# The two-input operations of GpSimd moved to VectorE, in a hybrid SSD and forgetting-attention block

## Chip, cores and metric

One core of a Trainium2 chip runs the whole layer in one launch. The metric is the device time of that launch in microseconds (us), the median of several runs. In the text PE is TensorE (matmuls), DVE is VectorE, ACT is ScalarE, POOL is GpSimd and SP is the SyncE queue that issues all DMAs.

## What is computed

Float32 throughout, one sequence of 1024 tokens, D = 1024. Cut to what matters:

```python
ada = silu(c) @ w_ada + b_ada;  shift, scale, gate = split(ada, 3)
h = rmsnorm(x, norm_w) * (1 + scale) + shift
z_ssm, xbc, dt_raw, q, k, v, z_att, f_logit, g_logit = split(h @ w_in)      # 8472 columns
# SSD branch: 16 heads of 64, 2 groups, state 64, chunks of 128 tokens
xs, bm, cm = split(silu(causal_conv(xbc)));  dt = softplus(dt_raw + dt_bias)
a_cs = cumsum(-exp(a_log) * dt) within a chunk
y = (cm bm^T * exp(a_cs[l] - a_cs[s])) (xs*dt)  +  cm state * exp(a_cs)  +  d_skip * xs
y_ssm = rmsnorm(y * silu(z_ssm), ssm_norm_w)
# attention branch: 8 heads of 128, causal, logits + f_cum[q] - f_cum[k]
y_att = softmax(q k^T * scale + forget) v * silu(z_att)
g_ssm, g_att = split(sigmoid(g_logit + b_gate))
merged = g_ssm * (y_ssm @ w_proj_ssm) + g_att * (y_att @ w_proj_att)
out = rmsnorm(x + gate * (merged @ w_out), final_norm_w)
```

## The kernel before

Every large product is made at nearly full float32 precision out of three matmuls. A tensor is *split* into a high part, which ScalarE casts (line 102), and a low part, raw minus high, a subtraction of two tensors in SBUF (line 103). Then high times high, high times low and low times high are summed in PSUM. `split(raw, hi, lo, n, eng)` takes the engine of the subtraction as an argument; in the kernel before its default is GpSimd. `unit` (line 87) loads a weight tile of 128 x 512 into one of four raw buffers (`wr`) and splits it into one of five `wh` and five `wl`.

The stages, in the order of time:

- **Start.** The tokens are normalised, the columns of w_ada are summed by VectorE (`ada_cols`, lines 287 and 289), and h is built, transposed and split into `hh` and `hl` (line 307). Three gate slabs fill TensorE meanwhile.
- **Half sums and pairs of slabs.** The columns of w_in come in slabs of 128. Two slabs at a time (`c_pair`, line 459) are multiplied with h in the manner of Strassen and Winograd: seven products instead of eight. `t_forms` (line 435) makes the sums and differences of h's halves once (`pe`, lines 440 to 444) and splits them (`tla`, `tlb`). For each pair VectorE forms four sums of weight tiles (lines 477 to 480), seven tiles are split (`wl`, and `sl` of three buffers), TensorE runs seven products of twelve matmuls, and VectorE adds the results up out of PSUM (lines 504 to 517). What follows depends on the slab: a tanh gate (`gt`, line 186), a silu (`zt`, line 525) or a causal convolution (`cv`, lines 538 to 544, four passes over 1024 columns on VectorE). Among the pairs a table, WPREP, places `w_sums` (line 575), which forms the weight sums of the later projections, and `out_gate` (lines 558 and 561), which forms the columns of the residual gate.
- **SSD.** Per quarter of the heads and chunk of 128 tokens (`ssd_half`, line 671): the decay matrix `ab` on ScalarE, its product with `cb` on VectorE (line 686), split into `m4`; xs transposed on TensorE, times dt (`xd`, line 700), times the decay (`xe`, line 703), both split into `xr`; the state `st32` updated (line 717) and split into `sn`; then the products. v and some q and k slabs run in between and fill TensorE.
- **Attention.** Per head and block of queries: logits on TensorE, the masked minimum on VectorE (line 1013), exp on ScalarE, normalisation on GpSimd (line 1021), transposes, split, product with v. GpSimd also selects the causal part (line 1004).
- **Projections.** `prod_c` runs three products (by w_proj_ssm, w_proj_att, w_out), again seven for eight, with `b_form` splitting the activations (`bl`), `w_in` (line 196) loading the weights, and `post` adding up. Sums of results (lines 1109 and 1126) and a product with the final norm's weight (line 1139) are GpSimd's. The end of each token block is a power on GpSimd (line 1144), two scalings and the store.

What sets the order: each engine runs its own queue in order, and a scheduler in the building layer puts the instructions of each queue into an order by its own estimate of when each can run, with a higher priority for the SSD and the attention. So an instruction that changes engine is put into the other queue where that estimate has it, and the order of the others can change with it. All DMAs are in SP's queue.

Which two-input operations were GpSimd's: every split whose call names no engine (the weights' `wl` and `sl`, `m4`, one half of `xr`, `sn`, v, spilled q and k), half of the sums and splits in `t_forms`, two sums and half of the gate products in `w_sums`, `xe`, the square sum `sacc` (line 778), and the sums and products named above. Two tables, WV and WVI (lines 54 and 55), gave some weight splits of the later projections to VectorE.

Of the kernel before, what the change touches and what calls it, by code (L numbers as in the profile page):

```python
# [27 lines left out]
ALU = mybir.AluOpType  # L28
# [25 lines left out]
WV = {'ps': (), 'pa': (1,), 'o': (1, 2, 3)}  # L54
WVI = (("o", 3),)
# [14 lines left out]
def build(ctx, tc, t):  # L70
# [16 lines left out]
    def unit(src, n, eng=G):  # L87
        raw = raw_tile()
        SP.dma_start(out=raw[:, :n], in_=src)
        return split(raw, hi_tile(), lo_tile(), n, eng)  # L90
# [10 lines left out]
    def split(raw, hi, lo, n, eng=G):  # L101
        A.copy(out=hi[:, :n], in_=raw[:, :n])  # L102
        eng.tensor_tensor(out=lo[:, :n], in0=raw[:, :n], in1=f32(hi[:, :n]), op=ALU.subtract)  # L103
        return hi, lo
# [91 lines left out]
    def w_in(n, i, p):  # L196
        if (n, i, p) in ws_scr:
            return unit(ws_scr[n, i, p], 512, V if p in WV[n] or (n, i) in WVI else G)
        return unit(t["w_" + n][p + 4 * (i == 4), i % 2 == 0 and 1 or 0], 512)
# [160 lines left out]
    with tc.tile_pool(name="pa", bufs=1, side="right") as pa, \  # L360
# [74 lines left out]
        def t_forms(k):  # L435
            th1, tl1, th2, tl2 = (pa.tile([P, S], F32R, name=f"t{n}{k}") for n in ("ha", "la", "hb", "lb"))
            b11, b12, b21, b22 = (pe_tile() for _ in range(4))
            lo, hi = slice(0, 512), slice(512, 1024)
            for b, kk, hs, eng in ((b11, k, lo, V), (b12, k, hi, G), (b22, k + 4, hi, G), (b21, k + 4, lo, V)):
                eng.tensor_tensor(out=b, in0=f32(hh[kk][:, hs]), in1=f32(hl[kk][:, hs]), op=ALU.add)  # L440
# [134 lines left out]
        def w_sums(n, p, gb=None):  # L575

            def raw_in(sl, u):
                x = raw_tile()[:, :512]
                SP.dma_start(out=x, in_=t["w_" + n][sl, u])
                if gb is not None:  # L580
                    (V if u else G).tensor_tensor(out=x, in0=x, in1=gb[:, 512 * (sl // 4):512 * (sl // 4) + 512],
                                                  op=ALU.mult)
                return x
# [4 lines left out]
            G.tensor_tensor(out=a21, in0=a11, in1=a21, op=ALU.subtract)  # L588
            G.tensor_tensor(out=s4, in0=a12, in1=s2, op=ALU.subtract)
# [40 lines left out]
    with tc.tile_pool(name="sd", bufs=1, side="right") as sd, \  # L630
# [40 lines left out]
        def ssd_half(qd, hf, xs, ys, st32, sn):  # L671
# [3 lines left out]
            for c in range(4 * hf, 4 * hf + 4):  # L675
# [25 lines left out]
                if c < NC - 1:  # L701
                    xe = sd.tile([P, 256], F32, tag="xe", bufs=2, name="xe")
                    G.tensor_tensor(out=h4(xe), in0=h4(xd), in1=hb4(dec), op=ALU.mult)
# [53 lines left out]
        for qd in range(4):  # L757
            st32, sn = sd.tile([P, 256], F32, tag="st32", bufs=1, name="st32"), None
            for hf in range(2):
# [7 lines left out]
                for i in range(2):  # L767
# [8 lines left out]
                    else:  # L776
                        A.activation(out=zt, in_=y, func=AF.Square)
                        G.tensor_tensor(out=sacc[:, hs], in0=sacc[:, hs], in1=zt, op=ALU.add)
# [75 lines left out]
    def b_t2(b11, b12, b22, b21=None):  # L854
# [5 lines left out]
        if b21 is not None:  # L860
            G.tensor_tensor(out=b21, in0=b21, in1=t2, op=ALU.subtract)
# [215 lines left out]
    with tc.tile_pool(name="finp", bufs=1, space=PSUM) as fpp_:  # L1077
# [9 lines left out]
        for i in OSSM:  # L1087
            if i in done_early:
                continue
            if i in (5, 4) and prep_u:  # L1090
                prep_u = False
                for p in range(4):
# [3 lines left out]
                    G.tensor_tensor(out=b[21][p], in0=b[21][p], in1=t2, op=ALU.subtract)  # L1096
# [8 lines left out]
        def att_done(ch, tk, p, ps):  # L1105
# [3 lines left out]
            G.tensor_tensor(out=m, in0=m, in1=gt, op=ALU.add)  # L1109
# [14 lines left out]
        def out_pre(hf, tk, p, st):  # L1124
            r = rt[4 * tk + p, hf]
            G.tensor_tensor(out=r, in0=r, in1=st, op=ALU.add)  # L1126

        def out_done(hf, tk, p, ps):
# [6 lines left out]
            if not last:  # L1135
# [3 lines left out]
                G.tensor_tensor(out=ra, in0=ra, in1=fw[:, hs], op=ALU.mult)  # L1139
# [101 lines left out]
```

## Time and profile before

| | |
|---|---|
| median of 3 runs | 1287.4 us (1284.27 to 1290.71) |
| profiled execution, its own time | 1286.09 us |
| its span | 1284.4 us |
| mean granted clock of TensorE | 0.974 |
| instructions of VectorE, GpSimd | 1618, 644 |

The span is that of one profiled execution; the rest of its time lies around it. A row of a group reads: line, engine, operation, what it writes and reads, shape, count, then busy time in all and the mean of one in ns, then the idle time of the engine just before these instructions and what ended it. Lines are those of the kernel before.

### The profile page before, as it was taken

Reading aid. Unit: us, or ns where it says so; the run is one execution under the profiler, and the core shown is the slowest. Engines: PE = TensorE matmul, PEld = TensorE weight load, DVE = VectorE, ACT = ScalarE, POOL = GpSimd, SP = SyncE. Lnnn points to the kernel's source line nnn. Section 1 sums busy time; section 2 is a strip of 40 time slices with the busy share of each in tenths; the row PEclk is TensorE's granted clock in tenths of the full one; section 3 lists DMA queues with packets and bytes.
Section 4 is the critical chain, followed back from the end, with each engine's and each line's share of the span. In section 5 each row is a group of like instructions: output and inputs, shape, how many; then the busy total and the mean of one; then the engine's idle time right before and its main releaser. Section 6 shows DMA issues by size and latency. Waiting matters only on the chain. (4 is left out here: it accounts for less than half of the span.)

```text
span 1284.4 us, 18783 instructions
## 1 busy us (share of the span) xinstructions
PE 1183.9 (92%) x6206; PEld 988.8 (77%) x6206; DVE 963.1 (75%) x1618; ACT 594.8 (46%) x1194; POOL 776.1 (60%) x644
## 2 busy tenths in 40 slices
PE   4897899999978999999988999999999999999896
PEld 3686688777766788799778888888887787878685
DVE  6979767787799566348689764545667968999997
ACT  5443324242423232477667733444456553444354
POOL 3258465474755476448887966435446635587666
PEclk9998899998989999999999999999999999999999
DMA  8422443624556566654565558623236619766143
GB/s 346 158 100 98 160 123 124 213 64 167 188 185 216 175 211 228 223 177 148 188 200 163 173 191 296 210 87 116 74 127 210 201 55 328 224 188 193 52 116 145
DMA packets 104126, 219.70 MB, mean 171 GB/s; under 512 B 11818, under 2 KB 19420, under 8 KB 103004
## 3 DMA queue, kind: packets, MB, share of 16 engines
q1 hardware_dynamic: 104028, 218.50, 51.5%
q8 instruction: 49, 0.80, 0.3%
q14 instruction: 49, 0.40, 0.1%
HBM read 154.85 MB, written 63.61 MB: 170 GB/s over the span
## 5 line engine op out<-in xcount | busy, mean ns | idle before, releaser
L103 POOL TENSOR_TENSOR wl<-wr,wh 128x512 fp32r<-128x512 f32 (+1 forms) x188 | 281.5, 1508 | 135.7 <-ACT wh L102 130.7
L102 ACT CAST wh<-wr 128x512 fp32r<-128x512 f32 (+1 forms) x214 | 129.8, 618 | 158.4 <-DMA wr<-w_c 53.7
L103 POOL TENSOR_TENSOR sl<-sr,sh 128x512 fp32r<-128x512 f32 x57 | 91.0, 1603 | 78.8 <-ACT sh L102 65.7
L115 PE MATMUL mm<-hh,wh 128*128 128x512 f32 x288 | 115.9, 407 | 4.3 <-ACT wh L102 1.9
L116 PE MATMUL mm<-hl,wh 128*128 128x512 f32 x288 | 116.7, 405 | 3.0 <-DVE hl L307 3.0
L117 PE MATMUL mm<-hh,wl 128*128 128x512 f32 x288 | 116.3, 405 | 0.0
L102 ACT CAST sh<-sr 128x512 fp32r<-128x512 f32 x57 | 34.1, 619 | 96.6 <-DVE sr L478 77.0
L140 PE MATMUL mm<-wh,hh 128*128 128x256 f32 (+1 forms) x256 | 74.9, 294 | 3.8 <-DVE tmp L348 3.8
L141 PE MATMUL mm<-wl,hh 128*128 128x256 f32 (+1 forms) x256 | 74.8, 293 | 0.0
L142 PE MATMUL mm<-wh,hl 128*128 128x256 f32 (+1 forms) x256 | 74.4, 292 | 0.0
L1018 ACT ACTIVATE pr<-pr,sm 128x1024 f32<-128x1024 f32 (+3 forms) x64 | 49.9, 780 | 50.4 <-DVE sm L1017 42.4
L1021 POOL TENSOR_SCALAR pr<-pr,sm 128x1024 f32<-128x1024 f32 (+3 forms) x64 | 48.6, 762 | 34.7 <-DVE sm L1020 30.2
L1013 DVE CUSTOM_DVE_ANT_0 pr<-lg,fb 128x512 f32<-128x512 f32 (+1 forms) x96 | 51.5, 551 | 23.5 <-PE lg L1012 14.0
L115 PEld LDWEIGHTS mm<-hh,wh 128*128 128x128 f32 x288 | 55.1, 193 | 15.6 <-ACT wh L102 2.4
L116 PEld LDWEIGHTS mm<-hl,wh 128*128 128x128 f32 x288 | 55.3, 192 | 14.7 <-DVE hl L307 3.9
L1004 POOL TENSOR_SCALAR_AFFINE_SELECT fb<-fb 128x128 f32<-128x128 f32 x64 | 21.9, 344 | 72.1 <-DVE sm L1013 57.3
L117 PEld LDWEIGHTS mm<-hh,wl 128*128 128x128 f32 x288 | 55.2, 192 | 10.8
L1037 DVE TENSOR_TENSOR ptl<-tp,pth 128x512 fp32r<-128x512 f32 (+1 forms) x80 | 50.1, 632 | 15.9 <-ACT pth L1036 15.5
L1036 ACT CAST pth<-tp 128x512 fp32r<-128x512 f32 (+1 forms) x80 | 42.3, 543 | 41.5 <-PE tp L1033 32.4
L683 ACT ACTIVATE ab<-ab,acs 128x128 f32<-128x128 f32 x128 | 41.1, 391 | 31.7 <-DMA ab<-a_scr 28.1
L140 PEld LDWEIGHTS mm<-wh,hh 128*128 128x128 f32 x256 | 49.5, 194 | 4.7 <-DVE tmp L348 4.5
L103 POOL TENSOR_TENSOR m<-ab,m 128x512 fp32r<-128x512 f32 x32 | 46.7, 1462 | 7.1 <-ACT m L102 4.7
(393 smaller groups left out, 3972.6 us busy)
## 6 DMA issues: line engine op xcount, KB each, us to landing
wr<-w_c SPq DMA_DIRECT2D x116, 256.0 KB, 3.5
wa<-w_ada SPq DMA_DIRECT2D x8, 1024.0 KB, 11.4
g_scr<-gt SPq DMA_DIRECT2D x16, 512.0 KB, 4.0
ab<-a_scr SPq DMA_DIRECT2D x32, 256.0 KB, 3.7
gt<-g_scr SPq DMA_DIRECT2D x32, 256.0 KB, 3.0
wr<-w_ps SPq DMA_DIRECT2D x28, 256.0 KB, 2.9
wr<-w_pa SPq DMA_DIRECT2D x28, 256.0 KB, 3.1
wr<-so SPq DMA_DIRECT2D x28, 256.0 KB, 2.6
```

What stands on the lines that cost most here:

```text
L102: A.copy(out=hi[:, :n], in_=raw[:, :n])
L103: eng.tensor_tensor(out=lo[:, :n], in0=raw[:, :n], in1=f32(hi[:, :n]), op=ALU.subtract)
L115: PE.matmul(ps, lhsT=hi[:, cs], rhs=xh[k][:, hs], start=(k == 0), stop=False)
L116: PE.matmul(ps, lhsT=hi[:, cs], rhs=xl[k][:, hs], start=False, stop=False)
L117: PE.matmul(ps, lhsT=lo[:, cs], rhs=xh[k][:, hs], start=False, stop=(k == 7))
L140: PE.matmul(o, lhsT=xh[k][:, ts], rhs=hi[:, cs], start=(k == 0), stop=False)
L141: PE.matmul(o, lhsT=xh[k][:, ts], rhs=lo[:, cs], start=False, stop=False)
L142: PE.matmul(o, lhsT=xl[k][:, ts], rhs=hi[:, cs], start=False, stop=(k == 7))
L1013: V.tensor_tensor_reduce(out=pr[:, n0:n1], in0=lg[:, :n1 - n0], in1=fb[:, n0:n1], op0=ALU.add, op1=ALU.min, scale=1.0, scalar=BIG, accum_o ...
L1018: A.activation(out=pr[:, :n], in_=pr[:, :n], func=AF.Exp, scale=-1.0, bias=sm[:, 0:1], accum_out=sm[:, 1:2])
L1021: G.tensor_scalar(out=pr[:, :n], in0=pr[:, :n], scalar1=sm[:, 1:2], scalar2=0.5, op0=ALU.mult, op1=ALU.mult)
L1037: V.tensor_tensor(out=ptl[:, :w], in0=tp[:, :w], in1=f32(pth[:, :w]), op=ALU.subtract)
```

## The change

Every `tensor_tensor` that GpSimd ran on two tensors in SBUF is given to VectorE. GpSimd keeps the causal selects, the powers with -0.5 and the normalisation of the attention's probabilities. No tile, buffer count, table of the schedule or DMA is changed. Cut to its core:

```diff
-WV = {'ps': (), 'pa': (1,), 'o': (1, 2, 3)}
-WVI = (("o", 3),)
...
-    def unit(src, n, eng=G):
+    def unit(src, n, eng=V):
...
-    def split(raw, hi, lo, n, eng=G):
+    def split(raw, hi, lo, n, eng=V):
         A.copy(out=hi[:, :n], in_=raw[:, :n])
         eng.tensor_tensor(out=lo[:, :n], in0=raw[:, :n], in1=f32(hi[:, :n]), op=ALU.subtract)
...
-            return unit(ws_scr[n, i, p], 512, V if p in WV[n] or (n, i) in WVI else G)
+            return unit(ws_scr[n, i, p], 512)
...
-            for b, kk, hs, eng in ((b11, k, lo, V), (b12, k, hi, G), (b22, k + 4, hi, G), (b21, k + 4, lo, V)):
+            for b, kk, hs, eng in ((b11, k, lo, V), (b12, k, hi, V), (b22, k + 4, hi, V), (b21, k + 4, lo, V)):
...
-            for b, th, tl, hs, eng in ((b11, th1, tl1, lo, V), (b12, th1, tl1, hi, G), (b22, th2, tl2, hi, V),
-                                       (b21, th2, tl2, lo, G)):
+            for b, th, tl, hs, eng in ((b11, th1, tl1, lo, V), (b12, th1, tl1, hi, V), (b22, th2, tl2, hi, V),
+                                       (b21, th2, tl2, lo, V)):
...
-                    (V if u else G).tensor_tensor(out=x, in0=x, in1=gb[:, 512 * (sl // 4):512 * (sl // 4) + 512],
+                    V.tensor_tensor(out=x, in0=x, in1=gb[:, 512 * (sl // 4):512 * (sl // 4) + 512],
...
-            G.tensor_tensor(out=a21, in0=a11, in1=a21, op=ALU.subtract)
-            G.tensor_tensor(out=s4, in0=a12, in1=s2, op=ALU.subtract)
+            V.tensor_tensor(out=a21, in0=a11, in1=a21, op=ALU.subtract)
+            V.tensor_tensor(out=s4, in0=a12, in1=s2, op=ALU.subtract)
...
-                    G.tensor_tensor(out=h4(xe), in0=h4(xd), in1=hb4(dec), op=ALU.mult)
+                    V.tensor_tensor(out=h4(xe), in0=h4(xd), in1=hb4(dec), op=ALU.mult)
...
-                        G.tensor_tensor(out=sacc[:, hs], in0=sacc[:, hs], in1=zt, op=ALU.add)
+                        V.tensor_tensor(out=sacc[:, hs], in0=sacc[:, hs], in1=zt, op=ALU.add)
...
-            G.tensor_tensor(out=m, in0=m, in1=gt, op=ALU.add)
+            V.tensor_tensor(out=m, in0=m, in1=gt, op=ALU.add)
...
-            G.tensor_tensor(out=r, in0=r, in1=st, op=ALU.add)
+            V.tensor_tensor(out=r, in0=r, in1=st, op=ALU.add)
...
-                G.tensor_tensor(out=ra, in0=ra, in1=fw[:, hs], op=ALU.mult)
+                V.tensor_tensor(out=ra, in0=ra, in1=fw[:, hs], op=ALU.mult)
```

Two subtractions from b21 (lines 861 and 1096) change in the same way. Since two lines fall away at the top, lines of the kernel after are smaller by two.

The order of the two programs shows 492 instructions fewer in GpSimd's queue and 492 more in VectorE's; the other queues hold the same instructions, not in the same order. Two places in VectorE's queue follow. The first is between two pairs of slabs at which `out_gate` runs as well. `sr` and `wr` are raw sums and raw weights of the next pair, `sl` and `wl` its low parts, `gb` the gate columns, `zt` the silu of the pair now in PSUM (`pp`, `mm`), `pe` its partial sums. Before:

```order
L561 SCALAR_TENSOR_TENSOR gb_3035<-wga_3208,cols_80,gb_3035 128x256
L478 TENSOR_TENSOR sr_3593<-sr_3592,wr_3584 128x512
L479 TENSOR_TENSOR wr_3586<-wr_3584,wr_3586 128x512
L558 TENSOR_SCALAR gb_3035<-wga_3391,cols_80 128x256
L480 TENSOR_TENSOR sr_3594<-wr_3590,sr_3593 128x512
L504 TENSOR_TENSOR pe_3461<-pp_3478,pe_3460 128x512
L561 SCALAR_TENSOR_TENSOR gb_3035<-wga_3391,cols_80,gb_3035 128x256 x3
L505 TENSOR_TENSOR pe_3462<-pp_3492,pe_3461 128x512
```

After, from the sum that line 480 made before:

```order
L478 TENSOR_TENSOR sr_3594<-wr_3590,sr_3593 128x512
L523 SCALAR_TENSOR_TENSOR zt_3214<-zt_3214,mm_3338 128x512
L523 SCALAR_TENSOR_TENSOR zt_3214<-zt_3214,pp_3354 128x512
L505 TENSOR_TENSOR pe_3463<-pp_3506,pe_3461 128x512
L101 TENSOR_TENSOR sl_3604<-sr_3593,sh_3603 128x512
L506 TENSOR_TENSOR pp_3506<-pp_3506,pe_3462 128x512
L101 TENSOR_TENSOR sl_3612<-sr_3592,sh_3611 128x512
L559 SCALAR_TENSOR_TENSOR gb_3035<-wga_3208,cols_80,gb_3035 128x256
L101 TENSOR_TENSOR wl_3608<-wr_3586,wh_3607 128x512
L101 TENSOR_TENSOR wl_3616<-wr_3588,wh_3615 128x512
L509 TENSOR_TENSOR mm_3523<-mm_3523,pe_3462 128x512
L101 TENSOR_TENSOR wl_3620<-wr_3590,wh_3619 128x512
```

The low parts of the next pair now stand between the additions out of PSUM (505, 506, 509) that free the banks of this pair.

The second place is a chunk of the SSD. `ab` is the decay matrix, `m4`, `xr` and `sn` are split operands, `st32` is the state, `ys` the output. Before:

```order
L686 TENSOR_TENSOR ab_5537<-ab_5537,cb0_4656 128x512
L717 SCALAR_TENSOR_TENSOR st32_5233<-st32_5233,ed_810,sp_5308 64x64 x4
L741 TENSOR_TENSOR ys_5238<-sp_5335,eb_5332 128x2x128
L700 TENSOR_TENSOR xd_5493<-xp_5489,dt_807 128x256
L744 TENSOR_TENSOR ys_5238<-sp_5319,ys_5238 64x2x128 x2
L103 TENSOR_TENSOR xr_5415<-xd_5416,xr_5415 128x256
L686 TENSOR_TENSOR ab_5595<-ab_5595,cb0_4656 128x512
```

After, from the same product to the next of its kind:

```order
L684 TENSOR_TENSOR ab_5537<-ab_5537,cb0_4656 128x512
L776 TENSOR_TENSOR sacc_4758<-sacc_4758,zt_5226 128x512
L101 TENSOR_TENSOR xr_5415<-xd_5416,xr_5415 128x256
L101 TENSOR_TENSOR sn_5316<-st32_5233,sn_5316 64x256
L739 TENSOR_TENSOR ys_5238<-sp_5335,eb_5332 128x2x128
L101 TENSOR_TENSOR xr_5415<-xe_5418,xr_5415 128x256
L698 TENSOR_TENSOR xd_5493<-xp_5489,dt_807 128x256
L715 SCALAR_TENSOR_TENSOR st32_5233<-st32_5233,ed_810,sp_5366 64x64 x4
L742 TENSOR_TENSOR ys_5238<-sp_5319,ys_5238 64x2x128 x2
L101 TENSOR_TENSOR wl_7324<-wr_7321,wh_7323 128x512
L701 TENSOR_TENSOR xe_5495<-xd_5493,dec_809 128x256
L684 TENSOR_TENSOR ab_5595<-ab_5595,cb0_4656 128x512
```

Of a chunk's chain, `sacc`, `sn`, the second half of `xr`, `xe` and a weight's `wl` have come in between two products with `cb`.

More of the change, by code (lines that the diff above doesn't have):

```diff
@@ L860, in b_t2 @@
         if b21 is not None:
-            G.tensor_tensor(out=b21, in0=b21, in1=t2, op=ALU.subtract)
+            V.tensor_tensor(out=b21, in0=b21, in1=t2, op=ALU.subtract)
         return f
@@ L1095, in build @@
                     V.tensor_tensor(out=t2, in0=b[22][p], in1=b[11][p], op=ALU.subtract)
-                    G.tensor_tensor(out=b[21][p], in0=b[21][p], in1=t2, op=ALU.subtract)
+                    V.tensor_tensor(out=b[21][p], in0=b[21][p], in1=t2, op=ALU.subtract)
             prod_c(i, "ps", b_form(i, b, lambda: raw_tile()[:, :512]), sx, su3, ssm_done)
```

## The prediction

> **What bounds the kernel now.** I read the page's first lines, then the busy time by stage, then VectorE's and GpSimd's rows in order of time, then the groups by shape within single stages, last TensorE's waits.
>
> ```profile
> span 1284.4 us, 18783 instructions
> ...
> PE 1183.9 (92%) x6206; PEld 988.8 (77%) x6206; DVE 963.1 (75%) x1618; ACT 594.8 (46%) x1194; POOL 776.1 (60%) x644
> ```
>
> TensorE (PE) is the bound: 1184 of 1284 us. What can be won is the 100 us in which it idles, and the time in which its clock is halved after idling. Where that is, the table of stages says (columns: stretch, its length, busy us of each engine with its instruction count, granted clock, DMA share, GB/s):
>
> ```profile
> 0.00:64.20 64.20, 41.21 (x172) 30.80 (x173) 51.78 (x114) 31.61 (x52) 19.19 (x24) 0.97 0.66 252
> 96.30:160.60 64.30, 51.73 (x222) 41.58 (x221) 55.80 (x81) 23.12 (x43) 42.37 (x28) 0.89 0.39 129
> 160.60:353.20 192.60, 186.28 (x778) 147.88 (x777) 145.96 (x165) 67.43 (x116) 116.03 (x72) 0.97 0.45 146
> 353.20:417.40 64.20, 51.41 (x213) 40.67 (x211) 61.83 (x78) 20.37 (x35) 38.33 (x25) 0.93 0.60 201
> 578.00:738.50 160.50, 147.78 (x1125) 133.14 (x1124) 129.18 (x263) 116.30 (x295) 136.21 (x126) 0.98 0.57 175
> 738.50:963.30 224.80, 223.04 (x1292) 192.85 (x1290) 123.06 (x325) 100.30 (x199) 112.48 (x128) 1.00 0.47 157
> 1059.60:1252.30 192.70, 183.11 (x778) 146.47 (x779) 187.21 (x216) 82.05 (x148) 130.58 (x84) 0.99 0.58 184
> 1252.30:1284.40 32.10, 21.52 (x94) 17.22 (x92) 24.13 (x43) 15.81 (x36) 20.01 (x18) 0.92 0.39 145
> ```
>
> The rows are: start; half sums t_forms with the first pair; pairs of slabs; the pairs in which out_gate runs; the SSD; attention; the three projections; the end. TensorE loses 12.6 us in the second (64.3 - 51.7) and 12.8 us in the fourth, where VectorE is busy 87% and 96%. The attention leaves 1.8 us of 224.8: nothing can be won there.
>
> But VectorE's "busy" is not all work. In the projections it first stands alone (upper fence), and shortly after beside GpSimd (the next fence VectorE, the last GpSimd; start, duration, instruction):
>
> ```profile
> 1237.12 0.68 DVE L103 TENSOR_TENSOR wl<-wr,wh 128x512 fp32r<-128x512 f32 x1
> 1237.72 0.68 DVE L103 TENSOR_TENSOR bl<-m,bh 128x512 fp32r<-128x512 f32 x1
> 1238.33 0.68 DVE L103 TENSOR_TENSOR wl<-wr,wh 128x512 fp32r<-128x512 f32 x1
> ```
> ```profile
> 1245.40 1.79 DVE L103 TENSOR_TENSOR wl<-wr,wh 128x512 fp32r<-128x512 f32 x1
> 1247.11 1.78 DVE L103 TENSOR_TENSOR bl<-m,bh 128x512 fp32r<-128x512 f32 x1
> 1248.82 1.79 DVE L103 TENSOR_TENSOR wl<-wr,wh 128x512 fp32r<-128x512 f32 x1
> ```
> ```profile
> 1246.60 1.74 POOL L103 TENSOR_TENSOR wl<-wr,wh 128x512 fp32r<-128x512 f32 x1
> 1248.30 5.16 POOL L1126 TENSOR_TENSOR b<-b,u 128x512 f32<-128x512 f32 x3
> ```
>
> Alone, a split of 512 columns starts every 0.60 us (its record of 0.68 overlaps the next by 0.08). Beside GpSimd both engines start one every 1.71 us, in lockstep. Two operations then take 1.71 us, which VectorE alone would do in 1.20. An operation with one input in PSUM isn't stretched, in whatever company:
>
> ```profile
> L517 DVE TENSOR_TENSOR pp<-pp,pe 128x512 f32<-128x512 f32 x12 | 8.3, 690 | 6.3 <-PE pp L497 6.3
> ```
>
> So it is two-input work in SBUF, on both engines at once, that stretches; and the change removes just that from GpSimd.
>
> **The change part by part.** By the order of the two programs 492 instructions leave GpSimd for VectorE; TensorE, ScalarE and the DMA queue keep the same instructions in another order. Each moved one costs VectorE 0.60 us at 512 columns. At 256 it costs 0.34: the record of 0.42 from PSUM (the xd row below) less the 0.08 of overlap. In return VectorE's stretched operations shrink to 0.68. Stage by stage:
>
> *96.3 to 160.6.* Groups of VectorE there (busy us, mean ns, idle before):
>
> ```profile
> L440 DVE TENSOR_TENSOR pe<-hh,hl 128x512 f32<-128x512 f32 x4 | 7.0, 1743 | 0.0
> L103 DVE TENSOR_TENSOR tlb<-pe,thb 128x512 fp32r<-128x512 f32 x3 | 5.2, 1733 | 0.0
> ```
>
> Seven operations, each 1.06 us too long: 7.4 us. The same subtraction over all groups of the stage gives me 25 us (the small ones of the dt chain are stretched like the large). Added are GpSimd's 28 at 0.60, 16.8 us. VectorE ends up 8 us shorter in a stage whose t_forms chain releases TensorE. I take -6, between -8 and +9 (the last if only the seven shrink: 16.8 - 7.4).
>
> *353.2 to 417.4*:
>
> ```profile
> L561 DVE SCALAR_TENSOR_TENSOR gb<-wga,cols,gb 128x256 f32<-128x256 f32 x25 | 20.2, 809 | 1.7 <-DMA wga<-w_gate 1.3
> L541 DVE SCALAR_TENSOR_TENSOR cv<-xp,cols,cv 128x1024 f32<-128x1024 f32 x6 | 10.7, 1812 | 0.0
> ```
>
> The 25 of out_gate could be about 0.42 as at any 256 columns: 25 x 0.39 = 9.8 us back; the convolutions some 3, the sums of the pairs and of w_sums another 3 to 6. Against 16 to 19 stand 25 x 0.60 = 15.0. VectorE is hardly relieved, but the stalls here are single long ones that its backlog makes (the first and third row of TensorE's waits: total, times, longest):
>
> ```profile
> PE mm L495 <- ACT gt L186: 11.2, 2, 7.3
> PE tp L302 <- DVE xt L263: 7.2, 2, 6.2
> PE mm L495 <- DVE zt L525: 6.8, 1, 6.8
> ```
>
> A PSUM bank comes free only after an addition of VectorE that stands behind stretched ones. I take -4 (0 to -13).
>
> *The SSD, 578 to 738.5*, GpSimd first, then VectorE:
>
> ```profile
> L103 POOL TENSOR_TENSOR m<-ab,m 128x512 fp32r<-128x512 f32 x28 | 41.0, 1464 | 6.5 <-ACT m L102 4.1 <-issue 1.9
> L103 POOL TENSOR_TENSOR wl<-wr,wh 128x512 fp32r<-128x512 f32 x16 | 22.7, 1429 | 1.6 <-ACT wh L102 1.4
> L103 POOL TENSOR_TENSOR xr<-xe,xr 128x256 fp32r<-128x256 f32 x25 | 21.6, 865 | 9.7 <-ACT xr L102 9.4
> L703 POOL TENSOR_TENSOR xe<-xd,dec 128x256 f32<-128x256 f32 x24 | 20.2, 843 | 1.0 <-DVE xd L700 0.3
> L103 POOL TENSOR_TENSOR sn<-st,sn 64x256 fp32r<-64x256 f32 x23 | 19.7, 856 | 5.1 <-ACT sn L102 3.5
> L778 POOL TENSOR_TENSOR sacc<-sacc,zt 128x512 f32<-128x512 f32 x10 | 13.7, 1368 | 0.5 <-ACT zt L777 0.2
> ```
> ```profile
> L686 DVE TENSOR_TENSOR ab<-ab,cb 128x512 f32<-128x512 f32 x28 | 29.7, 1061 | 14.0 <-ACT ab L685 11.4 <-POOL sn L103 2.3
> L103 DVE TENSOR_TENSOR xr<-xd,xr 128x256 fp32r<-128x256 f32 x28 | 23.4, 837 | 12.0 <-ACT xr L102 12.0
> ```
> ```profile
> L700 DVE TENSOR_TENSOR xd<-xp,dt 128x256 f32<-128x256 f32 x27 | 11.3, 417 | 0.6
> ```
>
> Added: (28 + 16 + 10) x 0.60 + (25 + 24 + 23) x 0.34 = 56.9 us. Given back: 28 x 0.38 + 28 x 0.42 = 22.4 from the two rows, some 8 more from the products with zt and dskip: 30 us. VectorE goes from 129 to 156 us of 160.5, or less as records overlap. Here it gets busier, though each link of the chain that was GpSimd's is shorter (0.86 becomes 0.42). I take +5; the bounds are -3 (the chain's gain alone) and +37 (worked out under the rivals).
>
> *The projections, 1059.6 to 1252.3*:
>
> ```profile
> L103 DVE TENSOR_TENSOR bl<-b,bh 128x512 fp32r<-128x512 f32 x32 | 36.1, 1152 | 0.0
> L103 DVE TENSOR_TENSOR wl<-wr,wh 128x512 fp32r<-128x512 f32 x21 | 25.4, 1210 | 0.0
> L103 DVE TENSOR_TENSOR bl<-m,bh 128x512 fp32r<-128x512 f32 x19 | 24.2, 1287 | 0.1
> ```
>
> Given back 32 x 0.47 + 21 x 0.53 + 19 x 0.61 = 37.8 us, and over the stage's other groups about 21 more: 59. Added 84 x 0.60 = 50.4. VectorE, busy 97% here, gains some 9 us, and TensorE has 9.6 us of idle to give: -5 (0 to -9; +13 if only the quoted rows shrink).
>
> *The rest.* Start -2: its 64 us hold the sum of w_ada, stretched by few splits. 160.6 to 353.2: -2 of 6.3 us of idle. Attention 0, covered by TensorE's own 223 of 224.8 us; were that cover gone, selects and normalisation would still run on GpSimd alone. End 0: after TensorE's last product the powers stay on GpSimd as they were. The clock was 0.89 and 0.93 in the two bad stages, 0.11 x 64.3 + 0.07 x 64.2 = 11.6 us; with a third of the stalls gone -4.
>
> [...]
>
> The queues: VectorE runs its queue in order. A moved split waits for ScalarE's cast of its high part, and behind it then stand the additions that free PSUM banks, for which TensorE waits. On GpSimd nothing of that kind stood behind. The other side of it is that raw buffers (wr, four) are freed sooner, so SP's loads, queued in order, start no later.
>
> Sum: -2 - 6 - 2 - 4 + 5 + 0 - 5 + 0 - 4 = **-18 us**. The profiled execution took 1286.1 us, 1.7 above its span and 1.3 below the median of 1287.4. On the median: 1287.4 - 18 = 1269.
>
> **The rivals.**
>
> *VectorE's queue waits for ScalarE, and the SSD becomes VectorE's (slower).* Work 156 us; the waits for ScalarE that VectorE has now, 11.4 + 12.0; those that it inherits from GpSimd's rows, 4.1 + 1.4 + 9.4 + 3.5 = 18.4. If none overlaps anything, 198 us instead of 160.5: +37. With the other terms' -23 that is 1301, and about 1312 if some of it also appears among the pairs. It decides from +23 in the SSD on. For it: VectorE's splits there already idle 12.0 us. Against: in the projections they idle 0.0 and 0.1, since work queued ahead hides the cast, and the SSD's queue gets fuller.
>
> *Nothing to measure.* In the four stages VectorE is given back some 25 + 17 + 30 + 59 = 131 us and takes on 139: its load stays, and TensorE, 92% busy, goes on as before: 1287. For it: the attention and half of the pairs are full already.
>
> *All stalls of that sort go.* TensorE's idle in the second to fifth and the seventh row is 12.6 + 6.3 + 12.8 + 12.7 + 9.6 = 54.0, with the clock's 11.6 together 65.6; two thirds of it is 44: 1243. For it: nearly every stretched record is GpSimd's doing. Against: some stalls are the DMA's, and the load stays.
>
> [...]
>
> That the change doesn't do what it says can be left aside: the order shows GpSimd's queue without the 492.
>
> **How the numbers follow.** Forecast 0.45 (own range 1258 to 1282), VectorE's queue 0.23, nothing 0.15, all stalls 0.14, no relief 0.03. A measurement of this kernel tells about 0.5%, 6.4 us, from no change. Faster than 1281: the forecast but for 0.03, and all stalls, 0.56. Within: 0.15 + 0.03 = 0.18. Slower: 0.26. The range leaves out about one in ten on either side: 1240 to 1312.
>
> **What would show it.** Right: VectorE's two-input records at 0.68 for 512 columns outside the attention; its busy time near 963 still; the waits on gt and zt shorter; TensorE's idle in the second, fourth and seventh stage down by 15 together; the SSD within a few us of 160. [...]

## The result, and the profile after

The kernel after takes 1249.88 us (median of 4 runs, 1248.80 to 1251.52); the kernel before took 1287.38 beside it. The ratio is 0.971, with a 95% interval of 0.968 to 0.974: 37.5 us less, where the sum said 18. One run of e1 below (1311.25 us) and one of the kernel before beside it (1832.96 us) were slow ones at a granted clock of 0.85 and 0.58, and no figure here uses them.

The first lines of the page of the kernel after:

```profile
span 1248.6 us, 18388 instructions
...
PE 1172.3 (94%) x6206; PEld 981.6 (79%) x6206; DVE 1040.7 (83%) x2110; ACT 596.5 (48%) x1194; POOL 88.9 (7%) x152
```

Against the page of before, TensorE's idle time (span less busy) went from 100.5 to 76.3 us. That is 24.2 of the 35.8 us of span. The other 11.6 are in its busy time, 1183.9 to 1172.3 with the same 6206 matmuls. The stages in which the granted clock rose (the second to the fourth rows below: 0.92, 0.90 and 0.96 became 1.00, 1.00 and 0.98) lost 13.5 us of busy time and the others gained 2, so I read it as a better clock. (Behind a stall of the kernel before, 7.3 us up to 381.5 us, the granted clock is 0.50 from 378.0 to 384.8 us; there TensorE starts a matmul every 0.43 us, ahead of the stall every 0.23.) VectorE is busy 77.6 us more.

Where it came from is read stage by stage. I cut both traces at the same events: the first sum of `t_forms` on VectorE, the start and end of the first pair of slabs, the end of the last pair, the end of the attention, TensorE's last product. The kernel before (stretch, length, busy us with counts, granted clock, DMA share, GB/s):

```profile
0.00:75.50 75.50, 52.51 (x234) 40.32 (x235) 55.12 (x122) 37.99 (x62) 19.19 (x24) 0.98 0.56 215
75.50:120.10 44.60, 37.30 (x229) 34.02 (x228) 42.59 (x42) 17.02 (x34) 36.90 (x23) 0.92 0.36 120
120.10:155.50 35.40, 29.32 (x116) 22.59 (x115) 29.98 (x53) 11.69 (x22) 19.91 (x14) 0.90 0.40 128
155.50:542.10 386.60, 364.32 (x1519) 290.21 (x1518) 280.41 (x347) 130.59 (x225) 232.05 (x153) 0.96 0.53 177
542.10:1061.20 519.10, 496.87 (x3252) 438.83 (x3250) 344.55 (x800) 299.66 (x670) 317.44 (x330) 0.99 0.51 164
1061.20:1273.80 212.60, 203.57 (x864) 162.86 (x864) 205.95 (x247) 93.72 (x175) 148.94 (x98) 0.99 0.55 176
1273.80:1284.40 10.60, 0.02 (x1) 0.00 (x0) 4.54 (x8) 4.11 (x8) 1.65 (x4) 0.75 0.67 250
```

The kernel after, in the same seven stages:

```profile
0.00:70.40 70.40, 51.35 (x234) 39.47 (x235) 51.38 (x131) 37.93 (x62) 6.15 (x15) 1.00 0.59 230
70.40:108.20 37.80, 37.80 (x250) 35.36 (x248) 36.68 (x70) 19.11 (x37) 0.00 (x0) 1.00 0.50 170
108.20:132.80 24.60, 21.08 (x93) 16.47 (x92) 24.03 (x59) 8.78 (x17) 0.00 (x0) 1.00 0.48 161
132.80:506.80 374.00, 358.51 (x1521) 285.89 (x1520) 320.68 (x504) 132.57 (x226) 0.00 (x0) 0.98 0.53 181
506.80:1028.30 521.50, 500.73 (x3251) 441.39 (x3249) 405.63 (x1001) 299.71 (x670) 78.11 (x129) 0.98 0.50 164
1028.30:1235.60 207.30, 202.85 (x864) 163.02 (x864) 195.98 (x336) 93.64 (x173) 2.25 (x4) 0.99 0.55 178
1235.60:1248.60 13.00, 0.00 (x0) 0.00 (x0) 6.33 (x13) 4.78 (x12) 2.40 (x4) 0.61 0.66 245
```

The differences are -5.1 (start), -6.8 and -10.8 (`t_forms`, first pair), -12.6 (the other 18 pairs), +2.4 (SSD and attention), -5.3 (projections), +2.4 (end): -35.8. So the gain lies among the pairs, and more than half of that in the 80 us of `t_forms` and the first pair. In those two rows VectorE does 129 instructions after instead of 95 before, and takes 60.7 us instead of 72.6.

That is the stretching going away. Groups of VectorE in that stretch, before (75.5 to 155.5 us):

```profile
L440 DVE TENSOR_TENSOR pe<-hh,hl 128x512 f32<-128x512 f32 x8 | 12.9, 1627 | 1.2 <-POOL tlb L103 1.1
L103 DVE TENSOR_TENSOR tlb<-pe,thb 128x512 fp32r<-128x512 f32 x4 | 7.0, 1742 | 0.0
```

and after (70.4 to 132.8 us):

```profile
L438 DVE TENSOR_TENSOR pe<-hh,hl 128x512 f32<-128x512 f32 x16 | 10.5, 685 | 0.1
L101 DVE TENSOR_TENSOR tlb<-pe,thb 128x512 fp32r<-128x512 f32 x8 | 5.3, 683 | 0.0
```

VectorE alone makes 16 of these sums in less time than it needed for 8 while GpSimd made the other 8. Nor did it inherit GpSimd's waits. In the SSD of the kernel after (506.8 to 736.8 us):

```profile
L101 DVE TENSOR_TENSOR m<-ab,m 128x512 fp32r<-128x512 f32 x32 | 21.9, 684 | 1.0 <-ACT m L100 0.6
L684 DVE TENSOR_TENSOR ab<-ab,cb 128x512 f32<-128x512 f32 x32 | 21.8, 685 | 4.6 <-ACT ab L683 4.4
...
L101 DVE TENSOR_TENSOR xr<-xd,xr 128x256 fp32r<-128x256 f32 x32 | 13.3, 416 | 1.2 <-ACT xr L100 1.2
L101 DVE TENSOR_TENSOR sn<-st,sn 64x256 fp32r<-64x256 f32 x28 | 11.8, 420 | 2.2 <-ACT sn L100 1.4
```

In a stretch of 160 us of before, the wait for ScalarE's cast of m was 4.1 us on GpSimd; in these 230 us it is 0.6 on VectorE. VectorE's own waits there, 11.4 for `ab` and 12.0 for `xr`, are 4.4 and 1.2.

What stays late among the pairs is in TensorE's waits (total, times, longest):

```profile
PE mm L493 <- DVE zt L523: 6.9, 1, 6.9
PE pp L568 <- DVE gb L559: 5.4, 1, 5.4
```

Both are in the pair at which two quarters of `out_gate` run (pair 12, counted from 0). It is the one pair that got longer by much, 27.3 to 33.9 us from its first product to the next pair's; an undisturbed one takes 19.4. The granted clock is 0.50 there from 374.9 to 391.8 us.

### The profile page after: what moved, and what is told of

Its sections match the earlier page's. It is cut to its first block, busy times and chain, and to the rows that moved or that the text cites. A ratio compares the mean times of both kernels' runs of the same rounds, so it can differ in the third digit from the quotient of the medians.

```text
span 1248.6 us, 18388 instructions
## 1 busy us (share of the span) xinstructions
PE 1172.3 (94%) x6206; PEld 981.6 (79%) x6206; DVE 1040.7 (83%) x2110; ACT 596.5 (48%) x1194; POOL 88.9 (7%) x152
## 4 chain that ended last, share of the span: by engine, by line
PE 58%; DVE 21%; DMA 10%; ACT 5%; issue 4%; SPq 0%; POOL 0%; DVEq 0%; ACTq 0%
PE pv L1041 4%; PE pp L493 4%; PE pp L495 4%; PE pp L494 4%; PE lg L1010 4%; PE mm L114 3%; PE mm L113 3%; PE mm L115 3%; DVE wl L101 3%; DMA ab<-a_scr 3%; PE tp L1031 2%; PE mm L493 2%; PE mm L495 2%; PE mm L494 2%; DMA wr<-w_c 2%
## 5 line engine op out<-in xcount | busy, mean ns | idle before, releaser
L101 DVE TENSOR_TENSOR wl<-wr,wh 128x512 fp32r<-128x512 f32 (+1 forms) x214 | 145.0, 690 | 15.2 <-ACT wh L100 14.2
L1011 DVE CUSTOM_DVE_ANT_0 pr<-lg,fb 128x512 f32<-128x512 f32 (+1 forms) x96 | 51.5, 551 | 19.5 <-PE lg L1010 14.8
L114 PEld LDWEIGHTS mm<-hl,wh 128*128 128x128 f32 x288 | 55.2, 192 | 11.4 <-DVE hl L305 0.9
L113 PEld LDWEIGHTS mm<-hh,wh 128*128 128x128 f32 x288 | 54.8, 192 | 10.8 <-ACT hh L304 0.9
L681 ACT ACTIVATE ab<-ab,acs 128x128 f32<-128x128 f32 x128 | 41.0, 391 | 45.9 <-DMA ab<-a_scr 37.0
L1019 POOL TENSOR_SCALAR pr<-pr,sm 128x1024 f32<-128x1024 f32 (+3 forms) x64 | 52.7, 825 | 78.4 <-DVE sm L1018 67.3
L902 PE MATMUL mm<-bh,wh 128*128 128x512 f32 x108 | 44.7, 417 | 4.3 <-ACT wh L100 2.6
L139 PEld LDWEIGHTS mm<-wl,hh 128*128 128x128 f32 x256 | 48.3, 189 | 0.2
L140 PEld LDWEIGHTS mm<-wh,hl 128*128 128x128 f32 x256 | 48.3, 189 | 0.0
## 6 DMA issues: line engine op xcount, KB each, us to landing
wa<-w_ada SPq DMA_DIRECT2D x8, 1024.0 KB, 11.4
```

Source lines behind the costliest of these rows:

```text
L113: PE.matmul(ps, lhsT=hi[:, cs], rhs=xh[k][:, hs], start=(k == 0), stop=False)
L114: PE.matmul(ps, lhsT=hi[:, cs], rhs=xl[k][:, hs], start=False, stop=False)
L139: PE.matmul(o, lhsT=xh[k][:, ts], rhs=lo[:, cs], start=False, stop=False)
L140: PE.matmul(o, lhsT=xl[k][:, ts], rhs=hi[:, cs], start=False, stop=(k == 7))
L1019: G.tensor_scalar(out=pr[:, :n], in0=pr[:, :n], scalar1=sm[:, 1:2], scalar2=0.5, op0=ALU.mult, op1=ALU.mult)
```

## The experiments

The theory: a two-input operation of VectorE in SBUF and one of GpSimd stretch each other, and the stretched queues of both made TensorE wait. Its rivals: the moved instructions are simply shorter on VectorE, or the saved hops between engines count (the chain theory); or the scheduler's new order did it. The first four kernels split the change in two and then put idle work on GpSimd.

**e1, the splits alone.** The change, with the sums, products and merges left on GpSimd; against the kernel after, lines of this kind:

```diff
-            V.tensor_tensor(out=a21, in0=a11, in1=a21, op=ALU.subtract)
+            G.tensor_tensor(out=a21, in0=a11, in1=a21, op=ALU.subtract)
```

> Of the change only the splits go to VectorE (some 360 of the 492 instructions); sums, products and merges stay on GpSimd. If stretching by two-input work on both engines is what cost the time, GpSimd keeps some 190 of its 700 us of such work and most of the 37 us should be won: 1253 to 1264 us. If the gain hangs on the sums at the head of a chain (half sums, weight sums), little of it is here: above 1270 us.

Measured: 1261.09 us (median of three runs, 1257.89 to 1262.67), ratio 0.979 (0.976 to 0.983).

**e2, the sums, products and merges alone.** The complement: the default of `split` and `unit` stays `eng=G`.

> The other part alone: sums, products and merges on VectorE, splits as in the kernel before. By the stretching, GpSimd still has over 500 us of two-input work: 1274 to 1288 us. If the chain heads are what matters: below 1265 us.

Measured: 1279.0 us (1276.18 to 1282.93), ratio 0.994 (0.991 to 0.996). From the first lines of the pages of e1 and of e2:

```profile
PE 1174.8 (94%) x6206; PEld 981.7 (78%) x6206; DVE 1040.1 (83%) x1976; ACT 597.9 (48%) x1194; POOL 275.3 (22%) x286
```
```profile
PE 1178.7 (92%) x6206; PEld 984.5 (77%) x6206; DVE 995.5 (78%) x1752; ACT 597.0 (47%) x1194; POOL 611.2 (48%) x510
```

Both parts gain, some 26 and 8 us, nearly the whole together, and both times are in the range that the stretching gave. In e1 VectorE is as busy as after with 134 instructions fewer: what GpSimd still does stretches it (its `wl` splits take 803 ns on average, 689 after).

By stage the two differ. The first pair takes 24.8 us in e1 and 34.2 in e2 (35.4 before, 24.6 after), and pair 11 19.4 and 28.6 (28.6 before, 21.0 after): what the pairs gain comes with the splits. The projections take 210.9 and 203.4 us (212.6 before, 207.3 after): their gain comes with the sums. SSD and attention take 526.0 and 531.3 us, against 519.1 before and 521.5 after (518.1 when that kernel ran again). So to give VectorE the sums and products of that chain without its splits, as e2 does, costs time there.

**e3, idle reads.** The kernel after, and GpSimd subtracts 112 columns of ones from themselves, four times behind every split of 512 columns that the program makes after the start (1452 in all). Nobody uses the result. The subtractions wait for nothing, so GpSimd runs the first of them at 1.6 us, beside the start. VectorE's order is that of the kernel after but for some 40 of its 2110 instructions, 8 of them up to the last pair.

```diff
+            for c in range(4):
+                G.tensor_tensor(out=junk, in0=ones[:, :112], in1=ones[:, :112], op=ALU.subtract)
```

> The kernel after, with some 1400 subtractions of 112 columns on GpSimd that nobody waits for and whose result nobody reads, from the end of the start onwards; VectorE's queue stays all but the same. If stretching is the cause: VectorE's splits of 512 columns go from 0.68 us to about 1.0 us up to some 480 us into the run, half sums and pairs get longer by 10 to 35 us, 1260 to 1285 us in all, and the SSD after that is as in the kernel after. If the gain came from the shorter duration of the moved instructions or from the scheduler's new order: 1250 us, within 4.

Measured: 1400.4 us, ratio 1.087 (1.084 to 1.091): the right direction, and far more than expected. The subtractions lasted to 922 us. The norm's power `rc` and the attention's first select stood behind them in GpSimd's queue:

```profile
799.62 91.41 POOL L112 TENSOR_TENSOR junk<-ones 128x112 f32<-128x112 f32 x198
890.99 1.65 POOL L798 TENSOR_TENSOR rc<-rc,mhalf 128x8 f32<-128x8 f32 x1
```

TensorE's first logits came 92.3 us after the SSD's end, 3.7 in the kernel after. That is my experiment's doing. The part free of it is `t_forms` and the pairs, which end at 547.2 us (506.8 after, 542.1 before). They are compared under e4.

**e4, idle writes.** The same with twice as many memsets, which read nothing:

```diff
+            for c in range(8):
+                G.memset(junk, 0.0)
```

> As the run before, with some 2800 memsets of 112 columns in place of the subtractions: GpSimd writes SBUF but reads nothing. If what stretches VectorE is GpSimd reading: 1250 us, within 4, and splits at 0.68 us. If any work of GpSimd does it: like the subtractions, 1260 us and more.

Measured: 1253.58 us, ratio 0.974 (0.970 to 0.977). VectorE's weight splits between 100 and 540 us, and GpSimd's idle work, first in e3, then in e4:

```profile
L101 DVE TENSOR_TENSOR wl<-wr,wh 128x512 fp32r<-128x512 f32 x79 | 62.8, 814 | 6.2 <-ACT wh L100 5.5 <-PE pp L505 0.7
...
L112 POOL TENSOR_TENSOR junk<-ones 128x112 f32<-128x112 f32 x1452 | 793.1, 546 | 112.5
```
```profile
L101 DVE TENSOR_TENSOR wl<-wr,wh 128x512 fp32r<-128x512 f32 x85 | 56.4, 685 | 7.3 <-ACT wh L100 6.5 <-PE pp L505 0.7
...
L112 POOL MEMSET junk<- 128x112 f32 x2904 | 569.8, 196 | 164.7
```

With 569.8 us of memsets on GpSimd a split takes 685 ns, as without them; with reads 814. It is not that GpSimd is busy that slows VectorE, but that it reads SBUF.

What this is worth to TensorE, from the first sum of `t_forms` to the end of the last pair, first in e3, then in e4:

```profile
78.70:547.20 468.50, 428.12 (x1860) 341.67 (x1860) 430.29 (x630) 160.13 (x280) 413.97 (x697) 0.95 0.49 166
```
```profile
73.50:510.70 437.20, 417.45 (x1861) 337.60 (x1860) 381.12 (x630) 160.27 (x280) 338.29 (x1726) 0.98 0.53 178
```

The same stretch took 466.6 us in the kernel before and takes 436.4 after. TensorE's order in it is that of the kernel after in both runs, and VectorE's but for a few instructions. So reads that nobody needs bring back what the change gained there, and writes do not. That they bring back the whole of it is partly luck, since these reads are other ones than those before.

**e8, reads that end early.** e3 without its fault: two subtractions behind each split instead of four, and none put behind the splits that come after the last pair. They ran from 1.6 to 204 us.

```diff
-            for c in range(4):
+            for c in range(2):
...
             fb()
+        late.clear()
```

> The kernel after, with GpSimd given idle subtractions of 112 columns (ones less ones, result never used) behind every split of 512 columns, two each, from t_forms to the last pair, and none after that, so that they are over before the SSD. Stretching by two-input reads: the first pair takes 30 us or more again and the pairs end at 525 to 545 us (506.8 after, 542.1 before), the SSD and all that follows keep the lengths of the kernel after, so 1268 to 1287. Rival (the gain comes from shorter chains on one engine or from the new order, and GpSimd's reads do no harm to what TensorE waits for): pairs end within 4 us of the kernel after, 1248 to 1255.

Measured: 1268.55 us (1268.07 to 1272.81), ratio 0.987 (0.984 to 0.989). The stages, cut as above:

```profile
0.00:79.20 79.20, 54.13 (x234) 40.31 (x235) 60.75 (x131) 38.06 (x62) 67.18 (x143) 0.98 0.54 205
79.20:117.80 38.60, 37.90 (x249) 35.27 (x248) 38.53 (x58) 17.47 (x35) 34.69 (x51) 1.00 0.47 156
117.80:154.30 36.50, 26.15 (x94) 19.00 (x94) 36.14 (x68) 9.62 (x19) 32.11 (x57) 0.81 0.36 113
154.30:528.60 374.30, 358.40 (x1521) 286.42 (x1520) 325.15 (x506) 133.14 (x227) 43.96 (x69) 0.98 0.54 181
528.60:1049.30 520.70, 499.94 (x3252) 441.62 (x3250) 404.22 (x1001) 300.17 (x670) 78.99 (x129) 0.98 0.50 164
```

The expectation was met: first pair over 30 us, last pair's end in the range, the time at its lower edge. The first pair ends at 154.3 us, 21.5 later than in the kernel after: 8.8 from the start, 0.8 from `t_forms` and 11.9 from the pair itself. (It ended at 155.5 before the change, but out of other parts: start, `t_forms` and first pair had been 5.1, 6.8 and 10.8 us longer. That the two ends agree is chance.) `t_forms` shows little because TensorE is busy nearly throughout it, 37.8 of 37.8 us after and 37.9 of 38.6 here. Nor do the reads harm the pairs beside which they end: in the 49.7 us from 154.3 to 204.0 TensorE does 216 matmuls without a pause, as in the 49.7 us behind the first pair of the kernel after; VectorE is busy 45.9 us of them instead of 43.6 and still keeps ahead. The two rows, e8 first:

```profile
154.30:204.00 49.70, 49.70 (x216) 39.98 (x215) 45.91 (x65) 21.83 (x36) 43.96 (x69) 1.00 0.45 149
```
```profile
132.80:182.50 49.70, 49.70 (x216) 40.01 (x215) 43.62 (x68) 21.63 (x35) 0.00 (x0) 1.00 0.45 153
```

So stretching costs time where VectorE has none to spare, as in the first pair (36.1 of 36.5 us busy).

All 18 other pairs together take 374.3 us (374.0 after), SSD and attention 520.7 (521.5). VectorE executes the same instructions, and up to the last pair in the same order but for 8 of 761; TensorE's order there is that of the kernel after but for one instruction moved in the start. So neither a new order nor longer chains between engines are needed to lose these 21.5 us: the reads alone do it.

**e6, `t_forms` alone given back.** The 16 instructions as before the change.

```diff
-            for b, kk, hs, eng in ((b11, k, lo, V), (b12, k, hi, V), (b22, k + 4, hi, V), (b21, k + 4, lo, V)):
+            for b, kk, hs, eng in ((b11, k, lo, V), (b12, k, hi, G), (b22, k + 4, hi, G), (b21, k + 4, lo, V)):
...
-            for b, th, tl, hs, eng in ((b11, th1, tl1, lo, V), (b12, th1, tl1, hi, V), (b22, th2, tl2, hi, V),
-                                       (b21, th2, tl2, lo, V)):
+            for b, th, tl, hs, eng in ((b11, th1, tl1, lo, V), (b12, th1, tl1, hi, G), (b22, th2, tl2, hi, V),
+                                       (b21, th2, tl2, lo, G)):
```

> The kernel after, with t_forms alone divided as before: GpSimd does two of its four sums and two of its four splits for each of the four k (16 instructions); all else stays on VectorE. The stretch from the first t_forms instruction to the end of the first pair went from 80.0 us (44.6 + 35.4) to 62.4 (37.8 + 24.6), where my term was -6. If t_forms' own stretching made all of it, the first pair ends 15 to 18 us later than in the kernel after and the time is 1263 to 1268. If, as the table of the prediction had it, t_forms is worth some 6 us and pair 0's own splits made the rest, t_forms takes 44 us, pair 0 stays at 25, and the time is 1254 to 1258. Rival (the halves of t_forms on two engines are quicker even when stretched, and only order and queue of the splits counted): 1245 to 1250.

Measured: 1259.58 us (1256.40 to 1268.02), ratio 0.980 (0.977 to 0.983). `t_forms` begins at 72.3 us (70.4 after) and takes 45.5 instead of 37.8; the first pair takes 23.3 instead of 24.6:

```profile
72.30:117.80 45.50, 41.21 (x250) 37.87 (x249) 44.95 (x56) 18.77 (x37) 25.57 (x15) 0.92 0.40 134
117.80:141.10 23.30, 21.46 (x96) 16.57 (x95) 22.14 (x55) 7.99 (x17) 1.68 (x1) 1.00 0.47 150
```

The two take 68.8 us, 6.4 more than the 62.4 of the kernel after. So of the 17.6 us that they gave with the change `t_forms`' own 16 instructions make 6.4; the other 11.2 belong to the other operations there, and by e1 and e2 to the splits above all. That is the second of the three expectations (44 and 25 us), with the median 1.6 us over the upper end of its time; the profiled run took 1256.40.

**e5, the SSD's chain alone given back.** The splits of m, of xe's half and of sn, `xe` and `sacc` on GpSimd, the fill work's splits on VectorE.

```diff
-                split(ab, m4[:, 0], m4[:, 1], 4)
+                split(ab, m4[:, 0], m4[:, 1], 4, G)
...
-                    split(xe, xr[:, 2], xr[:, 3], 256)
+                    split(xe, xr[:, 2], xr[:, 3], 256, G)
...
-                    split(st32[gs], sn[gs], sn[half[1 - g]], 256)
+                    split(st32[gs], sn[gs], sn[half[1 - g]], 256, G)
```

> The kernel after, with the SSD's own chain alone given back to GpSimd (the splits of m, xe's half of xr and sn, the product xe and the sum sacc, as before the change); everything else stays on VectorE. My term for the SSD was +5 and the stage measured +5.8 (227.9 to 233.7 us), while the gap from the SSD's end to the attention shrank from 11.7 to 3.7 us. If the SSD got longer because VectorE inherited this chain, the stage returns to about 228 us and the time is 1241 to 1247; if the gap comes back with it (GpSimd's power of the norm behind a longer queue), 1249 to 1255. Rival: the chain is better unstretched on one engine, and the longer SSD comes from the fill work's splits: then giving it back stretches VectorE's records again and the SSD takes 236 us or more, 1253 to 1265.

Measured: 1259.44 us (1257.73 to 1259.81), ratio 0.978 (0.976 to 0.981). SSD and attention, then two groups of the first 230 us in it:

```profile
509.30:1038.10 528.80, 502.33 (x3251) 440.07 (x3249) 378.78 (x871) 299.96 (x670) 213.09 (x259) 0.99 0.48 162
```
```profile
L684 DVE TENSOR_TENSOR ab<-ab,cb 128x512 f32<-128x512 f32 x32 | 31.6, 992 | 9.2 <-ACT ab L683 9.0
...
L101 DVE TENSOR_TENSOR wl<-wr,wh 128x512 fp32r<-128x512 f32 x25 | 20.4, 821 | 17.6 <-ACT wh L100 17.4
```

528.8 us against 521.5. The records stretch again (685 to 992 ns), and VectorE waits 17.4 us for `wh` where it waited 0.8. Taking this chain over was therefore a gain, 7 us by these two profiles and 8 to 10 by the medians (1249.88, and 1251.36 in e10 below), not the cost that I had put at +5. No expectation fits as a whole: the SSD by itself took 227.9 us before, 233.7 after and 232.4 here, neither 228 nor 236 and more, while the time lies in the rival's range. The gap to the first logits is 11.7, 3.7 and 11.7, and TensorE fills it with slabs of q and k. The order moves that work across the stage's edge, so only the two together say something. And e5 brings back the hops between the engines along with the stretching; which of them costs the 7 us it doesn't tell.

**e7, e9, e11: the remaining stall.** The engines of the kernel after, and the work at pair 12 spread by the table that places it. In e7, one quarter of `out_gate` (g) stands at each of the pairs 10 to 13, `gate_sum` (G) at 14, the fourth part of w_proj_att's sums (pa, 3) at 13. In e9 the third part goes to pair 8 and the fourth to 10; in e11 the third stays at 10 and the fourth goes to 5. The diff of e7:

```diff
-WPREP = {0: [('ps', 0)], 2: [('ps', 1)], 3: [('ps', 2)], 6: [('ps', 3), ('pa', 0)], 8: [('pa', 1)], 10: [('pa', 2), ('g', 0)], 12: [('pa', 3), ('g', 2), ('g', 3)], 11: [('g', 1)], 13: [('G', 0)], 15: [('o', 0)], 16: [('o', 1)], 17: [('o', 2)], 18: [('o', 3)]}
+WPREP = {0: [('ps', 0)], 2: [('ps', 1)], 3: [('ps', 2)], 6: [('ps', 3), ('pa', 0)], 8: [('pa', 1)], 10: [('pa', 2), ('g', 0)], 11: [('g', 1)], 12: [('g', 2)], 13: [('pa', 3), ('g', 3)], 14: [('G', 0)], 15: [('o', 0)], 16: [('o', 1)], 17: [('o', 2)], 18: [('o', 3)]}
```

> The kernel after, with the work ahead of the pairs spread evenly: out_gate's third quarter stays in pair 12, its fourth goes to pair 13, the sums of w_proj_att's last part to 13, and gate_sum from 13 to 14; the engines are those of the kernel after. Pair 12 is the one pair that got longer (27.3 to 33.9 us, an undisturbed one takes 19.4), with two stalls of TensorE of 5.4 and 6.9 us and the halved clock after them. If these stalls are VectorE's backlog from what is scheduled there, and can be dissolved, the pairs from 11 to 14 together take 8 to 13 us less: 1237 to 1242. Rival: the load is only moved, and another pair takes the stalls: 1247 to 1253.

> The spread kernel (e7) once more evened out: the sums of w_proj_att's third part go from pair 10 to pair 8 and those of its fourth from pair 13 to 10, both pairs of gate slabs, where VectorE has no product with zt and no convolution; out_gate's quarters stay in 10, 11, 12 and 13, gate_sum in 14. In e7 pair 13 takes 27.1 us with a stall of 5.8 on zt, pair 14 22.3, against 19.4 undisturbed. If that stall is VectorE's load in the pair, it goes: 1237 to 1241. Rival: the last backlog comes from out_gate itself, which waits for its loads and holds up what is queued behind: pairs 10 to 14 keep some 12 us over 19.4 each, 1244 to 1249.

> The spread kernel again, with the sums of w_proj_att's fourth part in pair 5, which had none, so that no pair holds two parts of w_sums that it did not hold in the kernel after; out_gate's quarters in pairs 10 to 13, gate_sum in 14. In the last one, two parts in pair 8 cost 23.8 and 27.2 us in pairs 7 and 8 (waits for ScalarE's wh and sh), while pairs 10 to 14 fell to 98.8 us against 109.0 in e7. If load per pair decides, both are had: pairs 5 to 9 near 100 us, 10 to 14 near 99, the time 1236 to 1241. Rival: a backlog appears wherever the fourth part goes, some 8 to 12 us: 1244 to 1249.

Beside e9 on its chip ran the kernel after once more (e10):

> The kernel after, unchanged, beside the spread one on the same chip: 1248 to 1252 under every theory; it is here so that a difference of 0.3 to 1% between the two can be told.

Measured: e7 1246.07 us (ratio 0.969, 0.966 to 0.971), e9 1246.60 (0.969, 0.967 to 0.971), e11 1249.42 (0.971, 0.968 to 0.973), e10 1251.36 (0.974, 0.971 to 0.976). Pairs 10 to 14 of the kernel after, and of e7:

```profile
311.50:428.80 117.30, 103.81 (x425) 81.29 (x424) 101.02 (x169) 38.26 (x68) 0.00 (x0) 0.93 0.51 176
```
```profile
310.60:419.60 109.00, 101.87 (x425) 80.73 (x425) 95.83 (x161) 35.15 (x62) 0.00 (x0) 0.97 0.55 189
```

The five pairs take 8.3 us less in e7 and 18.4 less in e9 (98.9). In e9 pairs 7 and 8 become 23.8 and 27.2; pair 8 holds the third part there beside the second, while the fourth, at pair 10, disturbs nothing (19.5). In e11 pair 6, behind the moved fourth part, takes 28.4. So a good part of the backlog goes where a part of the weight sums goes, as the rivals of e7 and e11 had it. The rival of e9, that `out_gate` itself makes it, fell with the 98.9, though the time came out in its range. The pairs 5 to 14 in all take 217.7, 208.8, 210.9 and 207.0 us (after, e7, e9, e11). None of the three times is in the range of its own theory, and little of these 7 to 11 us is left in the medians: e9 is 4.8 us, 0.4%, under the kernel after on the same chip, less than this measurement tells. I don't claim a version better than the change.

## Why the prediction was right in part, and where it failed

**The mechanism held.** Two-input reads of SBUF on both engines stretch both: in the lockstep rows VectorE's records go from 0.68 to 1.79 us and GpSimd's, 1.26 at the shortest (at 13.8 us), to 1.74. The change takes these reads from GpSimd, and VectorE's records shrink to 0.68 us. e3, e4 and e8 show it for `t_forms` and the pairs, where 30.2 of the 35.8 us lie; in the SSD and the projections no idle reads were tried by themselves. Waits for ScalarE didn't replace the stretching, as the SSD's rows show. On VectorE it needn't be two inputs: a product of `tmp` with a constant, 128x64 (line 370), took 1301 ns before and 189 after, and the scaling of `xt`, 128x1024 (line 263), up to 1815 ns before and at most 755 after.

**The step that failed: the size of what the pairs give back, -6 for `t_forms` with the first pair and -4 for the clock "with a third of the stalls gone".** By the stage rows, `t_forms` and the first pair gave 17.6 and the other pairs 12.6, in all 30.2 with the clock in it. My terms for the same, -6, -2, -4 and the clock's -4, make 16. That is 14.2 of the 17.8 us by which the sum missed the span's 35.8.

Three things were wrong in it. First, I counted VectorE's own books (25 us back, 17 added) and passed on a part. The -6 was argued from `t_forms`' chain, and e6 finds just that there, 6.4. What it left out is the first pair's own work, the other 11.2: VectorE is busy 30.0 of its 35.4 us before and 24.0 of 24.6 after, so I read the pair as bound by VectorE's pace, and its weight splits stood before on GpSimd, stretched as well. There the two engines together are what to cost. Two operations took 1.71 us in lockstep, and take 1.20 on VectorE; scaled so, the first pair's 35.4 would be 24.8, and 24.6 was measured. `t_forms`' 44.6 would be 31.3 against 37.8 measured, but there TensorE itself is busy all of the 37.8. This reckoning was made after the result and on one stretch.

Second, the stalls here did not shrink by a third but by three quarters: TensorE's idle time in the two rows went from 13.4 to 3.5 us, and the granted clock from 0.92 and 0.90 to 1.00. Over the kernel TensorE's busy time, in which I read the clock, fell by 11.6 us where I had 4 for the clock, and its idle time by 24.2, not 14.

Third, my table of stages passed over three stretches, 64.2 to 96.3, 417.4 to 578.0 and 963.3 to 1059.6 us, and had no term for them and no reason for that. The last pair lies in the second of them and became 3.8 us shorter.

**-2 and -4 for the other pairs were misplaced as well.** Pairs 10 to 14, with `out_gate`, took 117.6 us before and 117.3 after: nothing for the -4. The gain is in pairs 6 to 8, 70.6 to 61.2 us, in pair 11, 28.6 to 21.0, and in the last one, 23.5 to 19.7. What pair 11 won, pair 12 lost again. e9 and e11 show stalls that follow the load placed at each pair.

**The SSD's +5 and the attention's 0** are +2.4 together. That the size is near is luck: its reason fell with e5, where the moved chain gave 7 us back. Nor can +2.4 be told from chance: the kernel after took 518.1 us for the two when it ran again (e10). What keeps the stage near 520 us nevertheless is not settled; the order of the fill work changed with it.

**Projections -5:** -5.3, and -7.4 in e10; by e1 and e2 it hangs on the sums and not on the splits that my rows showed. **Start -2:** -5.1, of which 2.3 may be chance: the first sum of `t_forms` came at 70.4 us in the kernel after and at 72.7 when it ran again (e10). **End 0:** +2.4. Its row shows 13 instructions of VectorE behind the last product, 8 before; no run tried it.

**VectorE "near 963 still"** became 1040.7: my two sums, 131 back and 139 added, cover four stages and 263 of the 492 instructions. The 229 others add load too.

**The rivals.** *VectorE's queue waits for ScalarE* was wrong: the SSD's waits fell. *Nothing* was wrong. *All stalls of that sort go*, 1243, was nearer than the forecast; what spoke against it, that the load stays, did not matter: VectorE's busy time even rose by 77.6 us. I read it so that a stall ends with the pace of the queue and not with its load; no run tried that by itself. *No relief* (0.03; the moved load counts in full and VectorE's own operations give nothing back) was wrong: in the projections, where VectorE was busy 97%, taking work back made the stage 5.3 us shorter, and the kernel became 2.9% faster.

## What to carry to other kernels

Where two engines stretch each other, cost the pair: time both as they run together, time one alone with all the work, and scale by that ratio the stretches that end on either of them, down to where the next engine takes over; a balance of one engine's busy time doesn't see it. This fitted the first pair here and needs trying elsewhere. A stall removed near TensorE can be worth more than its length, since the granted clock rose with it: here 11.6 us of busy time beside 24.2 of idle. To prove such a contention, put unused work of the suspected sort on the idle engine, and in another run work without the suspected access; bound it in time, so that its own queue doesn't hold up what comes later. Where a change has parts, read each part's run by stage: e2's 8 us were a gain in three stages and a loss of 12 us in the SSD and attention.

## What the runs showed of the hardware

- GpSimd's memsets leave VectorE's two-input operations at 685 ns; GpSimd's reads stretch them, short ones of 112 columns too. These subtractions took 546 to 569 ns each on average, and VectorE's splits 814 to 832 ns beside them, against 1742 beside reads of 512 columns.
- GpSimd's busy share alone doesn't give the stretching: the sums of `t_forms` took 830 ns each in e8, 1627 before, with GpSimd busy 89% of `t_forms` and the first pair in e8 and 71% before. GpSimd's reads beside them had 112 columns in e8 (569 ns each on average over the run) and 512 before (1640 ns each for its own half of these sums); other lengths were not tried.
- Stretching alone costs no time where VectorE keeps ahead: in e8 TensorE did 216 matmuls in 49.7 us beside the reads, as without them.
